# A decoder trunk's first attention on one core: TensorE's order written by hand as a pipeline over heads

## The chip, the core and the metric

The kernel runs on one core of a Trainium2 chip. Its engines work side by side, each on a list of instructions of its own: TensorE (PE) multiplies, VectorE (DVE) and ScalarE (ACT) do arithmetic on tiles, GpSimd (POOL) a little masking, and SyncE (SP) issues most DMAs. An instruction starts when those ahead of it on its engine have been issued and the semaphores that it waits for have been signalled. The metric is the device time of one execution in microseconds, lower is better.

## What is computed

One sequence of 256 tokens with 2048 features goes through two layers. Layer 0 is an attention with 32 heads of 128 that sees only the 64 best keys of each query, layer 1 a stick-breaking attention with 16 heads; behind each stands an MLP of 8192. Each of the four parts is normalised ahead and behind, shifted, scaled and gated by columns that are computed from `c` with the large weight `ada_w`. Of the reference, cut to the first attention:

```python
q_lat, c_kv, k_idx, w_idx = jnp.split(proj, [c1, c2, c3], axis=-1)   # 512, 256, 128, 16 columns
q = (q_lat @ w_qb).reshape(B, S, A_HEADS, A_QK_DIM)
q_idx = (q_lat @ w_idx_qb).reshape(B, S, IDX_HEADS, IDX_DIM)
...
score = jnp.einsum('bqsh,bqh->bqs', jax.nn.relu(dots), wb).astype(jnp.float32)
score = jnp.where(key_pos[None, None, :] <= t[None, :, None], score, -jnp.inf)
_, idx = lax.top_k(score, k_top)                                      # k_top = 64
...
logits = jnp.einsum('bqhc,bqkc->bqhk', q_abs, kv_sel).astype(jnp.float32) * scale
logits = logits + jnp.moveaxis(rel_bias[bucket], -1, 2).astype(jnp.float32)
probs = jax.nn.softmax(logits, axis=-1).astype(h.dtype)
o_lat = jnp.einsum('bqhk,bqkc->bqhc', probs, kv_sel)
return jnp.einsum('bqhc,hcv->bqhv', o_lat, w_uv)                      # then @ w_out
```

## The kernel before, in words

**Products.** Every product of fp32 values is made as three: each operand is split into a high part (ACT rounds it, L128) and a low part (DVE subtracts, L129), and high by high, low by high and high by low are added in one PSUM bank. Weights come as raw tiles of 512 KB in a ring of four (`raw`) and are split into `whi` and `wlo`, rings of four too. Beside this a `Filler` streams most of `ada_w` through DVE: each `tick` makes the steps that are due, an add of 128x1024 to `acc` (L205) or one of the "ends": a gate (two products, L244 and L245, into a bank of the tag `s`, then DVE multiplies, L246) or four transposes of columns (`col`, L215). The tag `s` has one bank, which `pT`, the gates and `col` share; `lg` has two, `av` one.

**Start.** 2048 features come in groups; `start_sum` adds the weighted rows of `ada_w` on DVE, for the last three steps one row on PE as one-column products into `col`; the column sums (L565) end a group, and then h of its features can be made (L438, L439) and multiplied with `a_w_in` (`pq`, `pk`, L602).

**Mask.** Index scores are made in `dots`; DVE then takes eight maxima at a time and strikes them out (L889, L890), eight rounds for each of the two query tiles, L891 makes the mask, POOL cuts it (L893), PE transposes it (`mt`, L899), and DVE copies it (L900). Every head's logits add the mask by products with it (L839).

**Heads.** Four heads are a group, `hq` from 0 to 7. `a_project(hq)` makes their queries (`pqT`), keys (`pkT`) and values (`pv`). `a_attend` does one head: logits `lg` (L836 two products, L839 three), bias and maximum on DVE (L844), exponentials on ACT (L849), reciprocal on DVE (L851), scaling on ACT (L854), three transposes `pT` (L857), their copy on ACT (L859), products with v, `av` (L862, L863), and the split of the result. `a_out(hq - 1, d)` makes a quarter of the output projection of the group before: 24 products `m` of 512 columns (L353 to L355), whose sum DVE adds to `y` (L387).

**Who sets the order.** At the start PE's order is written by hand (`manual_schedule`); from the first attention on, a scheduler places the instructions of every engine by the order in which the code asks for them and by its own costs. So `projected = a_project(0)` and the loop over `hq` and `hl` state what there is to do, and not where on PE it comes to stand. The second attention (`b_attend`) makes its logits in the banks `z`, waits for `e`, its exponentials, at L1076, and puts its products with v into a bank of the tag `s` (`po`, named `bo`).

Of the kernel before, what the change touches and what calls it, by code (L numbers as in the profile page):

```python
# [16 lines left out]
P = 128  # L17
# [26 lines left out]
def trunk(ctx: ExitStack, tc: tile.TileContext, x, c, rel_bias, ada_w, ada_b, norm_g, a_w_in, a_q_norm,  # L44
# [74 lines left out]
    def rows(w, k0, k1, c0, c1):  # L119
        return w.rearrange("(a p) n -> p a n", p=P)[:, k0:k1, c0:c1]  # L120
# [127 lines left out]
    class Filler:  # L248
# [61 lines left out]
        def tick(self, weight=1):  # L310
            self.due += self.per * weight
            while self.due >= 1.0:
                self.due -= 1.0
                if self.done < self.limit:
                    self.step()
# [231 lines left out]
    def start_sum(i):  # L547
        g, k, r = steps[i]
        n = SEGS[g][1]
        on_pe = 1 if i >= len(steps) - 3 else 0  # L550
# [57 lines left out]
    for i in range(len(steps) + LEAD):  # L608
# [19 lines left out]
        if waiting and not (waiting[0] in late and done < len(steps) - 3):  # L628
            for k in waiting[:1 if SEGS[g][1] == 4 else 2]:
                waiting.pop(0)  # L630
                for t in range(NT):
                    start_product(oq, (k,), t)
                    if k not in late:
                        start_product(ok, (k,), t)
        if done == 2:
            x_sums = [squares(t) for t in range(NT)]
        if done == 4:
            start_x(x_sums)
        if done == 9:
            ps = small_ps("tab", "col")  # L640
            nc.tensor.matmul(ps[:HA, :3 * P], rb, bk, start=True, stop=True)
            nc.scalar.activation(tab, ps[:HA, :3 * P], AF.Copy)
            nc.gpsimd.dma_start(out=tab_d, in_=tab)
    start_h(len(SEGS) - 1)
    waiting += range(SEGS[-1][0], NC)
# [140 lines left out]
    def a_project(hq):  # L786

        qparts = unit(rows(a_w_qb[0], 0, 4, hq * BLK, (hq + 1) * BLK), 4, BLK)
        khi, klo = a_kv_unit(uk_src, hq)
        vhi, vlo = a_kv_unit(uv_src, hq)  # L790
        qk = []
        for a in range(2):
            pf = bank("f", "pqT")
            s_piece([(k, hi[:, a * 2 * P:(a + 1) * 2 * P], lo[:, a * 2 * P:(a + 1) * 2 * P])
                     for k, (hi, lo) in enumerate(qparts)], q_of, 2, [pf], 4)
            qT = q_tile[:, hq % 2, a].rearrange("p (a t) -> p a t", a=2)
            nc.scalar.activation(qT, pf.rearrange("p (a t) -> p a t", a=2), AF.Copy, scale=QS)
# [7 lines left out]
            kT = k_tile[:, hq % 2, a].rearrange("p (a t) -> p a t", a=2)  # L805
            nc.scalar.activation(kT, pf.rearrange("p (a t) -> p a t", a=2), AF.Copy)
            qk.append((qT, kT))
        vt = []
# [3 lines left out]
        for t in range(NT):  # L812
            v = v_tile[:, hq % 2, t]
            nc.scalar.activation(v, pv[t], AF.Copy)  # L814
            vt.append(v)
        return qk, vt
# [3 lines left out]
    def a_attend(hq, hl, qk, vt):  # L820

        a, b = divmod(hl, 2)
# [3 lines left out]
        if b == 0:  # L826
# [3 lines left out]
            o_tile[0] = pair_tile((11, 16, 17, 18, 10)[(2 * hq + a) % 5], "o")  # L830
# [21 lines left out]
        for t in range(NT):  # L852
            f, _ = krng[t]
            nc.scalar.activation(lg[:, f], lg[:, f], AF.Copy, scale=rc[:, t:t + 1])  # L854
        ps = small_ps("pT")
# [3 lines left out]
        nc.scalar.activation(pT, ps[:, :3 * P], AF.Copy)  # L859
        ps = small_ps("av", "av")  # L860
        hs = slice(hl * P, (hl + 1) * P)
        nc.tensor.matmul(ps[:, :T], vt[1][:, hs], pT[:, :T], start=True, stop=False, **kw)  # L862
        nc.tensor.matmul(ps[:, P:T], vt[0][:, hs], pT[:, T:], start=False, stop=True, **kw)  # L863
        o = o_tile[0][:, b]
# [15 lines left out]
    projected = a_project(0)  # L880
# [28 lines left out]
    for hq in range(8):  # L909
        ready, projected = projected, a_project(hq + 1) if hq < 7 else None  # L910
        for hl in range(4):
            a_attend(hq, hl, *ready)
            if hq > 0:
                a_out(hq - 1, hl)
# [142 lines left out]
    def b_attend(hq, pair):  # L1057
# [22 lines left out]
        for hl, (z, e) in enumerate(zip(zs, es), pair[0]):  # L1080
            nc.scalar.activation(e, z[:, :3 * P], AF.Exp)
            po = small_ps("bo")
# [91 lines left out]
```

## Time and profile before

| | |
|---|---|
| median of 3 runs | 2440.35 us (2436.56 to 2444.9) |
| the profiled execution | 2439.51 us, its span 2437.8 |
| PE busy | 2346.0 us of the span (96%), 12320 products |
| DVE, ACT, POOL busy | 1747.3, 1229.2 and 42.5 us |

A profile shows one execution. The busy time of an engine is the sum of its records; products overlap in PE's pipeline, so a busy PE is not a PE at its peak. The start lasts until about 130 us, the mask is ready at about 205, the first attention lasts until 512, the second from about 1300 to 1690, and the MLPs fill the rest.

### The profile page before, as it was taken

Reading aid. Unit: us, or ns where it says so; the run is one execution under the profiler, and the core shown is the slowest. Engines: PE = TensorE matmul, PEld = TensorE weight load, DVE = VectorE, ACT = ScalarE, POOL = GpSimd, SP = SyncE. Lnnn points to the kernel's source line nnn. Section 1 sums busy time; section 2 is a strip of 40 time slices with the busy share of each in tenths; the row PEclk is TensorE's granted clock in tenths of the full one; section 3 lists DMA queues with packets and bytes.
Section 4 is the critical chain, followed back from the end, with each engine's and each line's share of the span. In section 5 each row is a group of like instructions: output and inputs, shape, how many; then the busy total and the mean of one; then the engine's idle time right before and its main releaser. Section 6 shows DMA issues by size and latency. Waiting matters only on the chain.

```text
span 2437.8 us, 32909 instructions
## 1 busy us (share of the span) xinstructions
PE 2346.0 (96%) x12320; PEld 1954.0 (80%) x12320; DVE 1747.3 (72%) x2221; ACT 1229.2 (50%) x1847; POOL 42.5 (2%) x74
## 2 busy tenths in 40 slices
PE   3899999999999999999999999999999999999998
PEld 2487787868888888888878988987788888888886
DVE  6789798888576876876578677887865558555556
ACT  3156555566544444445455554456654454454443
POOL 0010000000000000000000000000000000000000
PEclk9899999999999999999999999999999999999999
DMA  9987899858677877877657778895765557656554
GB/s 379 369 287 249 271 310 308 284 190 280 226 266 244 302 266 264 306 258 270 194 181 265 255 264 318 308 332 210 243 241 190 190 186 263 207 190 190 182 191 145
DMA packets 285976, 613.94 MB, mean 252 GB/s; under 512 B 19716, under 2 KB 44632, under 8 KB 285304
## 3 DMA queue, kind: packets, MB, share of 16 engines
q1 hardware_dynamic: 282688, 603.14, 72.1%
q0 software_dynamic: 2464, 8.53, 1.2%
q8 instruction: 96, 1.57, 0.2%
q14 instruction: 64, 0.52, 0.1%
q10 hardware_dynamic: 664, 0.17, 0.0%
HBM read 609.62 MB, written 2.15 MB: 251 GB/s over the span
## 4 chain that ended last, share of the span: by engine, by line
PE 78%; DMA 8%; DVE 4%; ACT 4%; issue 4%; SPq 0%; POOL 0%; DVEq 0%; POOLq 0%; ACTq 0%
PE f L944 18%; PE m L354 11%; PE m L355 11%; PE m L353 11%; PE f L946 9%; DMA w<-in_ada_w_dram 3%; DVE acc L205 1%; DMA raw<-in_a_w_out_dram 1%; DMA adaw<-in_ada_w_dram 1%; PE pv L353 1%; PE pv L354 1%; PE pv L355 1%; ACT whi L128 1%; PE pq L123 1%; PE pq L125 1%
## 5 line engine op out<-in xcount | busy, mean ns | idle before, releaser
L129 DVE TENSOR_TENSOR wlo<-raw,whi 128x1024 fp32r<-128x1024 f32 x726 | 875.9, 1221 | 423.3 <-ACT whi L128 420.8
L128 ACT ACTIVATE whi<-raw 128x1024 fp32r<-128x1024 f32 x726 | 755.7, 1056 | 800.8 <-PE f L944 311.9
L944 PE MATMUL f<-h,whi 128*128 128x512 f32 x1920 | 676.0, 394 | 0.0
L946 PE MATMUL f<-h,wlo 128*128 128x256 f32 x1920 | 543.2, 283 | 0.8 <-DVE wlo L129 0.8
L944 PEld LDWEIGHTS f<-h,whi 128*128 128x128 f32 x1920 | 360.6, 188 | 82.5
L205 DVE SCALAR_TENSOR_TENSOR acc<-adaw,cs,acc 128x1024 f32<-128x1024 f32 x300 | 384.3, 1281 | 55.0 <-DMA adaw<-in_ada_w_dram 52.1
L353 PE MATMUL m<-whi,hid 128*128 128x512 f32 x1016 | 401.4, 395 | 0.0
L355 PE MATMUL m<-wlo,hid 128*128 128x512 f32 x1016 | 401.0, 395 | 0.0
L354 PE MATMUL m<-whi,hid 128*128 128x512 f32 x1016 | 400.9, 395 | 0.0
L946 PEld LDWEIGHTS f<-h,wlo 128*128 128x128 f32 x1920 | 360.9, 188 | 2.6 <-DVE wlo L129 1.4
L355 PEld LDWEIGHTS m<-wlo,hid 128*128 128x128 f32 x1016 | 191.3, 188 | 44.6
L353 PEld LDWEIGHTS m<-whi,hid 128*128 128x128 f32 x1016 | 191.4, 188 | 44.2
L354 PEld LDWEIGHTS m<-whi,hid 128*128 128x128 f32 x1016 | 191.4, 188 | 43.1
L387 DVE TENSOR_TENSOR y<-m,y 128x512 f32<-128x512 f32 x200 | 136.8, 686 | 37.9 <-PE m L355 37.6
L353 PE MATMUL m<-whi,o 128*128 128x512 f32 x368 | 149.4, 407 | 0.5 <-ACT qkv L814 0.5
L355 PE MATMUL m<-wlo,o 128*128 128x512 f32 x368 | 146.7, 401 | 0.4 <-DVE wlo L129 0.4
L354 PE MATMUL m<-whi,o 128*128 128x512 f32 x368 | 146.7, 399 | 0.0
L205 DVE SCALAR_TENSOR_TENSOR acc<-w,cs,acc 128x512 f32<-128x512 f32 (+1 forms) x87 | 81.4, 936 | 22.9 <-DMA w<-in_ada_w_dram 20.2
L355 PEld LDWEIGHTS m<-wlo,o 128*128 128x128 f32 x368 | 69.3, 189 | 15.6 <-DVE wlo L129 1.1
L353 PEld LDWEIGHTS m<-whi,o 128*128 128x128 f32 x368 | 69.6, 189 | 13.9 <-ACT qkv L814 0.7
L354 PEld LDWEIGHTS m<-whi,o 128*128 128x128 f32 x368 | 69.5, 189 | 13.5
L123 PE MATMUL pk<-h,whi 128*128 128x256 f32 x256 | 72.8, 285 | 1.0 <-ACT q L1052 1.0
(278 smaller groups left out, 2908.2 us busy)
## 6 DMA issues: line engine op xcount, KB each, us to landing
raw<-in_mlp_w_dram SPq DMA_DIRECT2D x504, 512.0 KB, 4.4
adaw<-in_ada_w_dram SPq DMA_DIRECT2D x320, 512.0 KB, 6.2
raw<-in_b_w_in_dram SPq DMA_DIRECT2D x92, 512.0 KB, 5.3
raw<-in_a_w_out_dram SPq DMA_DIRECT2D x64, 512.0 KB, 5.8
w<-in_ada_w_dram SPq DMA_DIRECT2D x62, 512.0 KB, 9.5
raw<-in_b_w_out_dram SPq DMA_DIRECT2D x32, 512.0 KB, 7.6
raw<-in_a_w_qb_dram SPq DMA_DIRECT2D x16, 512.0 KB, 5.8
win<-in_a_w_in_dram SPq DMA_DIRECT2D x8, 912.0 KB, 9.0
```

Source lines behind the costliest of these rows:

```text
L123: nc.tensor.matmul(o, sh, mh, start=start, stop=False, skip_group_check=True)
L125: nc.tensor.matmul(o, sl, mh, start=False, stop=stop, skip_group_check=True)
L128: return (nc.scalar.activation(dst_hi, src, AF.Copy).ins, nc.vector.tensor_sub(dst_lo, src, dst_hi.bitcast(F32)).ins)
L129: nc.vector.tensor_sub(dst_lo, src, dst_hi.bitcast(F32)).ins)
L205: nc.vector.scalar_tensor_tensor(acc, w, cs[:, k:k + 1], acc, op0=ALU.mult, op1=ALU.add)
L353: nc.tensor.matmul(o, xh[:, ts_], hi, start=(k == 0), stop=False)
L354: nc.tensor.matmul(o, xl[:, ts_], hi, start=False, stop=False)
L355: nc.tensor.matmul(o, xh[:, ts_], lo, start=False, stop=(k == n - 1))
L387: nc.vector.tensor_add(y, pt[d][t], y)
L944: nc.tensor.matmul(pf[f], hi[:, fs], hb.rearrange("p a t -> p (a t)"), start=(u == 0 and i == 0), stop=False, skip_group_check=True)
L946: nc.tensor.matmul(pf[f][:, :T], lo[:, fs], hb[:, 0], start=False, stop=(u == 3 and i == 3), skip_group_check=True)
```

## The change

Ahead of the mask and of the loop PE's order is now written by hand (`manual_schedule` for PE alone, until the last output piece of the loop): products stand on PE exactly in the order in which the code asks for them. `a_project` and `a_attend` became generators: a projection has three parts (queries of the group, then keys, then values), a head has three (logits and softmax, transposes, products with v). The loop takes one head after another: logits of head n+1, transposes of head n, an output piece of the group before (or a part of the projection, where none is left), products of head n with v, a part of the projection. Beside it, a `tick` of the `Filler` makes at most one end; of the last three steps of the start only the first and the last leave a row to PE; some q products of the start stand behind the last column sums; the pair tile of a head is taken later; and in the second attention `po` is the bank `z`.

```diff
 
         def tick(self, weight=1):
             self.due += self.per * weight
-            while self.due >= 1.0:
+            begun = self.done
+            while self.due >= 1.0 and self.done < self.limit:
+                if self.steps[self.done][3] >= NC and self.done > begun:
+                    break
                 self.due -= 1.0
-                if self.done < self.limit:
-                    self.step()
+                self.step()
 
         def finish(self):
             while self.done < self.limit:
...
     def start_sum(i):
         g, k, r = steps[i]
         n = SEGS[g][1]
-        on_pe = 1 if i >= len(steps) - 3 else 0
+        on_pe = 1 if i in (len(steps) - 3, len(steps) - 1) else 0
         if k == 0:
             acc[g] = (sp.tile([P, 2 * BLK], F32, tag="acc", name=uid("acc"), bufs=2)[:, :2 * n * P],
                       bank("col", "col"))
...
             start_h(g - 1)
             waiting += range(SEGS[g - 1][0], sum(SEGS[g - 1]))
         if waiting and not (waiting[0] in late and done < len(steps) - 3):
-            for k in waiting[:1 if SEGS[g][1] == 4 else 2]:
+            for k in waiting[:1 if SEGS[g][1] == 4 or waiting[0] in late else 2]:
                 waiting.pop(0)
                 for t in range(NT):
                     start_product(oq, (k,), t)
                     if k not in late:
                         start_product(ok, (k,), t)
+            if done >= len(steps) - 3:
+                held, waiting = waiting, []
         if done == 2:
             x_sums = [squares(t) for t in range(NT)]
         if done == 4:
...
             nc.tensor.matmul(ps[:HA, :3 * P], rb, bk, start=True, stop=True)
             nc.scalar.activation(tab, ps[:HA, :3 * P], AF.Copy)
             nc.gpsimd.dma_start(out=tab_d, in_=tab)
+    for t in range(NT):
+        start_product(oq, held, t)
     start_h(len(SEGS) - 1)
-    waiting += range(SEGS[-1][0], NC)
+    waiting = range(SEGS[-1][0], NC)
     for t in range(NT):
         start_product(oq, waiting, t)
     idx_unit = lambda u: rows(a_w_idx_qb[0], 0, 4, u * BLK, (u + 1) * BLK)
...
 
     def a_project(hq):
 
-        qparts = unit(rows(a_w_qb[0], 0, 4, hq * BLK, (hq + 1) * BLK), 4, BLK)
+        both = lambda pf: pf.rearrange("p (a t) -> p a t", a=2)
+        qk, vt = ([], []), []
+        parts = unit(rows(a_w_qb[0], 0, 4, hq * BLK, (hq + 1) * BLK), 4, BLK)
+        pf = [bank("f", "pqT") for _ in range(2)]
+        s_piece([(k, hi, lo) for k, (hi, lo) in enumerate(parts)], q_of, 4, pf, 4)
+        for a in range(2):
+            qk[0].append(both(q_tile[:, hq % 2, a]))
+            nc.scalar.activation(qk[0][a], both(pf[a]), AF.Copy, scale=QS)
+        yield
         khi, klo = a_kv_unit(uk_src, hq)
-        vhi, vlo = a_kv_unit(uv_src, hq)
-        qk = []
         for a in range(2):
-            pf = bank("f", "pqT")
-            s_piece([(k, hi[:, a * 2 * P:(a + 1) * 2 * P], lo[:, a * 2 * P:(a + 1) * 2 * P])
-                     for k, (hi, lo) in enumerate(qparts)], q_of, 2, [pf], 4)
-            qT = q_tile[:, hq % 2, a].rearrange("p (a t) -> p a t", a=2)
-            nc.scalar.activation(qT, pf.rearrange("p (a t) -> p a t", a=2), AF.Copy, scale=QS)
             pf = bank("f", "pkT")
             for b in range(2):
                 for k in range(2):
...
         for t in range(NT):
             f, _ = krng[t]
             nc.scalar.activation(lg[:, f], lg[:, f], AF.Copy, scale=rc[:, t:t + 1])
+        yield
         ps = small_ps("pT")
         for i, j in enumerate((0, 2, 1)):
             nc.tensor.transpose(ps[:, i * P:(i + 1) * P], lg[:, j * P:(j + 1) * P], ident)
         pT = pT_tile[:, hl % 2, :3 * P]
         nc.scalar.activation(pT, ps[:, :3 * P], AF.Copy)
+        yield
         ps = small_ps("av", "av")
         hs = slice(hl * P, (hl + 1) * P)
         nc.tensor.matmul(ps[:, :T], vt[1][:, hs], pT[:, :T], start=True, stop=False, **kw)
         nc.tensor.matmul(ps[:, P:T], vt[0][:, hs], pT[:, T:], start=False, stop=True, **kw)
+        if b == 0:
+            o_tile[0] = pair_tile((11, 16, 17, 18, 10)[(2 * hq + a) % 5], "o")
         o = o_tile[0][:, b]
         split(o[:, 0], o[:, 1], ps[:, :T])
         o_tiles[hq].append(o)
...
     def o_of(tiles):
         return lambda k: (tiles[k][:, 0], tiles[k][:, 1])
 
-    projected = a_project(0)
+    projected = {}
+    attention_order = ExitStack()
+    attention_order.enter_context(tc.manual_schedule(engines={mybir.EngineType.PE}))
+    for _ in a_project(0):
+        pass
+    project = a_project(1)
+    next(project), next(project)
 
     for s in (slice(0, P), slice(2 * P, 3 * P)):
         nc.gpsimd.affine_select(out=score[:, s], in_=score[:, s], pattern=[[-1, P]], compare_op=ALU.is_ge,
...
         out_part(a_w_out[0], 4 * q, 4, o_of(o_tiles[q]), yt, gates.get((0, 2)), ss, d, q == 0, q == 7,
                  ("x", "f", "m")[-len(d):], **kw)
 
-    for hq in range(8):
-        ready, projected = projected, a_project(hq + 1) if hq < 7 else None
-        for hl in range(4):
-            a_attend(hq, hl, *ready)
-            if hq > 0:
-                a_out(hq - 1, hl)
+
+    heads = [divmod(h, 4) for h in range(32)]
+    outs = []
+    before = None
+    for hq, hl in heads + [(8, 0)]:
+        now = a_attend(hq, hl) if hq < 8 else None
+        if now:
+            next(now)
+        if before:
+            next(before)
+        if outs:
+            a_out(*outs.pop(0))
+        else:
+            next(project, None)
+        if before:
+            next(before, None)
+        next(project, None)
+        if hl == 0 and hq > 0:
+            outs += [(hq - 1, d) for d in range(NB)] if hq < 8 else []
+        if hl == 3:
+            for _ in project:
+                pass
+            project = a_project(hq + 2) if hq < 6 else iter(())
+        before = now
+    for o_ in outs:
+        a_out(*o_)
+    attention_order.close()
     filler.finish()
     a_out(7, 0)
     early = {}
...
         oo = pair_tile(8 + hq % 2 * 2 + pair[0] // 2, "o")
         for hl, (z, e) in enumerate(zip(zs, es), pair[0]):
             nc.scalar.activation(e, z[:, :3 * P], AF.Exp)
-            po = small_ps("bo")
+            po = z
             hs = slice(hl * P, (hl + 1) * P)
             nc.tensor.matmul(po[:, :T], vt[0][:, hs], e[:, :T], start=True, stop=False, **kw)
             nc.tensor.matmul(po[:, P:T], vt[1][:, hs], e[:, T:], start=False, stop=True, **kw)
```

Three places show how PE's list moves. The names are those of the program (`pqT` queries and `pkT` keys of a group, `lg` logits, `pT` transposes, `av` products with v, `gate` an end of the `Filler`, `m` output), with tile numbers; line numbers of the kernel after are larger by 2 to 16.

The first place is on PE at the mask's transposes `mt`. Before:

```order
L124 MATMUL pqT_1729<-qlat,whi_1660 128x256
L125 MATMUL pqT_1729<-qlat,wlo_1661 128x256
L899 LDWEIGHTS misc
L899 MATMUL mt_1369<-ident_b,misc 128x128
L899 LDWEIGHTS misc
L899 MATMUL mt_1369<-ident_b,misc 128x128
L899 LDWEIGHTS misc
L899 MATMUL mt_1369<-ident_b,misc 128x128
L123 MATMUL pqT_1729<-qlat,whi_1664 128x256
```

and after:

```order
L124 MATMUL pkT_1411<-ckv_711,whi_1384 128x256
L125 MATMUL pkT_1411<-ckv_711,wlo_1385 128x256
L915 LDWEIGHTS misc
L915 MATMUL mt_1486<-ident_b,misc 128x128
L915 LDWEIGHTS misc
L915 MATMUL mt_1486<-ident_b,misc 128x128
L915 LDWEIGHTS misc
L915 MATMUL mt_1486<-ident_b,misc 128x128
L842 MATMUL lg_1503<-qkv_709,qkv_708 128x128
```

Before, the transposes stand in the midst of the third group's queries (`hq` 2), 42 products of which are ahead of them; after, they stand right behind the second group's keys (`hq` 1), and the logits of head 0 follow.

The second place is on PE in the first heads, which have no output piece beside them. Before, from the transposes of head 1 on:

```order
L857 MATMUL pT_1583<-ident,lg_716 128x128 x3
L862 MATMUL av_1588<-lg_717,qkv_713 128x256
L863 MATMUL av_1588<-lg_717,qkv_713 128x128
L857 MATMUL pT_1611<-ident,lg_716 128x128 x3
L836 MATMUL lg_1863<-qkv_712,qkv_711 128x128
L836 MATMUL lg_1863<-qkv_712,qkv_711 128x256
L839 LDWEIGHTS misc
L839 MATMUL lg_1863<-big_flip,misc 128x128
L839 LDWEIGHTS misc
```

and after, from the transposes of head 0 on:

```order
L864 MATMUL pT_1564<-ident,lg_713 128x128 x3
L870 MATMUL av_1569<-lg_714,qkv_710 128x256
L871 MATMUL av_1569<-lg_714,qkv_710 128x128
L244 MATMUL gate_1575<-ahl_1529,ones_r 128x256
L245 MATMUL gate_1575<-ahl_1529,ones_r 128x256
L842 MATMUL lg_1583<-qkv_709,qkv_708 128x128
L842 MATMUL lg_1583<-qkv_709,qkv_708 128x256
L845 LDWEIGHTS misc
L845 MATMUL lg_1583<-big_flip,misc 128x128
L845 LDWEIGHTS misc
L845 MATMUL lg_1583<-big_flip,misc 128x128
L845 LDWEIGHTS misc
```

Before, the logits of heads 2 and 3 stand further ahead, and two heads' transposes follow each other closely; after, one head's transposes and its products with v are neighbours, with the next head's logits behind them.

The third place is on PE where a `gate` meets an attention head, in the third group. Before:

```order
L354 MATMUL m_2286<-whi_2275,o_1936 128x512
L355 MATMUL m_2286<-wlo_2276,o_1936 128x512
L862 MATMUL av_2255<-lg_717,qkv_713 128x256
L863 MATMUL av_2255<-lg_717,qkv_713 128x128
L244 MATMUL gate_2260<-ahl_2132,ones_r 128x256
L245 MATMUL gate_2260<-ahl_2132,ones_r 128x256
L836 MATMUL lg_2313<-qkv_712,qkv_711 128x128
```

and after, twice:

```order
L845 MATMUL lg_2176<-big_flip,misc 128x128
L864 MATMUL pT_2192<-ident,lg_713 128x128 x3
L244 MATMUL gate_2211<-ahl_2121,ones_r 128x256
L245 MATMUL gate_2211<-ahl_2121,ones_r 128x256
L355 MATMUL m_2218<-whi_2201,o_1847 128x512
```

```order
L870 MATMUL av_2246<-lg_714,qkv_710 128x256
L871 MATMUL av_2246<-lg_714,qkv_710 128x128
L244 MATMUL gate_2252<-ahl_2215,ones_r 128x256
L245 MATMUL gate_2252<-ahl_2215,ones_r 128x256
L244 MATMUL gate_2265<-ahl_2256,ones_r 128x256
L245 MATMUL gate_2265<-ahl_2256,ones_r 128x256
L123 MATMUL pkT_2272<-ckv_711,whi_2261 128x256
```

Before, the gate stands behind `av`; after, one stands right behind `pT`, in whose bank it writes, and two stand behind each other.

## Rows read from the trace of the kernel before

**Rows 1.** The page's busy times: us (share of the span) x instructions.

```profile
PE 2346.0 (96%) x12320; PEld 1954.0 (80%) x12320; DVE 1747.3 (72%) x2221; ACT 1229.2 (50%) x1847; POOL 42.5 (2%) x74
```

**Rows 2.** Windows: stretch, length, each engine's busy time, granted clock, DMA share, GB/s.

```profile
178.00:204.60 26.60, 25.05 (x181) 23.14 (x179) 25.64 (x64) 15.56 (x22) 0.30 (x2) 1.00 0.77 265
204.60:223.30 18.70, 15.94 (x104) 12.83 (x104) 15.55 (x46) 14.73 (x41) 2.73 (x5) 1.00 0.51 154
223.30:512.00 288.70, 279.51 (x1527) 230.20 (x1527) 250.86 (x426) 169.94 (x346) 8.37 (x12) 1.00 0.87 297
555.00:1260.00 705.00, 705.00 (x3531) 593.71 (x3530) 507.69 (x553) 342.04 (x439) 2.02 (x4) 1.00 0.76 262
1300.00:1690.00 390.00, 380.68 (x2487) 344.75 (x2486) 296.35 (x311) 195.30 (x246) 2.11 (x5) 1.00 0.83 294
```

**Rows 3.** The timeline at the mask: start, duration, engine, line, out<-in [idle before].

```profile
203.87 0.36 DVE L891 TENSOR_SCALAR misc<-misc 128x384 bf16<-128x384 f32 x1
...
204.65 0.53 PE L899 MATMUL mt<-ident_b,misc 128*128 128x128 bf16 x3 [1.25 <-POOL misc L893]
```

**Rows 4.** Waits of PE, 223.3 to 512: us in total, times, longest.

```profile
PE av L862 <- ACT lg L859: 2.9, 5, 1.1
PE pT L857 <- ACT lg L854: 2.7, 5, 1.5
...
PE col L215 <- DVE mod L216: 0.6, 1, 0.6
```

**Rows 5.** PE's timeline behind the mask.

```profile
205.19 0.28 PE L124 MATMUL pqT<-qlat,whi 128*128 128x256 f32 x1
...
205.31 0.28 PE L125 MATMUL pqT<-qlat,wlo 128*128 128x256 f32 x1
...
211.30 0.40 PE L353 MATMUL pv<-whi,ckv 128*128 128x512 f32 x1
211.53 0.39 PE L354 MATMUL pv<-whi,ckv 128*128 128x512 f32 x1
...
223.25 0.50 PE L353 MATMUL m<-whi,o 128*128 128x512 f32 x1 [0.47 <-ACT qkv L814]
```

**Rows 6.** The timeline of one head, later in the first attention.

```profile
289.92 0.29 DVE L844 CUSTOM_DVE_ANT_0 lg<-lg,bias 128x128 f32<-128x128 f32 x1
...
290.48 1.22 DVE L129 TENSOR_TENSOR wlo<-raw,whi 128x1024 fp32r<-128x1024 f32 x1
...
291.81 0.40 ACT L849 ACTIVATE lg<-lg,st 128x128 f32<-128x128 f32 x1 [2.27 <-DVE st L846]
...
293.07 0.81 ACT L854 ACTIVATE lg<-lg,rc 128x128 f32<-128x128 f32 x2 [0.27 <-DVE rc L851]
...
293.73 0.27 PE L857 MATMUL pT<-ident,lg 128*128 128x128 f32 x1
...
294.08 0.38 PE L857 MATMUL pT<-ident,lg 128*128 128x128 f32 x2
...
294.90 0.47 ACT L859 ACTIVATE lg<-pT 128x384 f32<-128x384 f32 x1
```

**Rows 7.** The granted clock: two windows (columns as in rows 2).

```profile
72.10:75.20 3.10, 0.00 (x0) 0.00 (x0) 2.35 (x4) 2.95 (x9) 0.00 (x0) 1.00 1.09 386
75.60:79.00 3.40, 3.40 (x5) 1.55 (x6) 3.26 (x6) 0.19 (x1) 0.00 (x0) 0.50 1.09 389
```

**Rows 8.** The timeline at the end of the start.

```profile
112.09 3.90 DVE L205 SCALAR_TENSOR_TENSOR acc<-w,cs,acc 128x512 f32<-128x512 f32 x5 [0.92 <-DMA w<-in_ada_w_dram]
112.48 5.38 PE L602 MATMUL pq<-win,h 128*128 128x512 f32 x8
...
120.76 0.16 DVE L587 SCALAR_TENSOR_TENSOR mod_start<-col,g_col 128x2 f32<-128x2 f32 x1 [4.77 <-PE col L565]
...
121.62 1.22 PE L602 MATMUL pq<-win,h 128*128 128x512 f32 x1 [0.91 <-DVE h L439]
```

**Rows 9.** Waits of PE in the second attention, 1300 to 1690 (columns as in rows 4).

```profile
PE z L1076 <- DVE e L1075: 8.2, 8, 2.3
```

More of the change, by code (lines that the diff above doesn't have):

```diff
@@ L804, in a_project @@
                         xh, xl, start=(b == 0 and k == 0), stop=(k == 1))
[L805 to L808, printed above, removed]
+            qk[1].append(both(k_tile[:, hq % 2, a]))
+            nc.scalar.activation(qk[1][a], both(pf), AF.Copy)
+        yield
+        vhi, vlo = a_kv_unit(uv_src, hq)
         pv = [bank("m", "pv") for _ in range(NT)]
@@ L812, in a_project, with a_attend @@
         for t in range(NT):
[L813 to L816, printed above, removed]
+            vt.append(v_tile[:, hq % 2, t])
+            nc.scalar.activation(vt[t], pv[t], AF.Copy)
+        projected[hq] = list(zip(*qk)), vt
     biases, o_tile = {}, {}
-    def a_attend(hq, hl, qk, vt):
+    def a_attend(hq, hl):
+        qk, vt = projected[hq]
         a, b = divmod(hl, 2)
@@ L829, in a_attend @@
                                                                  ap=[[1, P], [3 * P, 2], [1, T]]))
-            o_tile[0] = pair_tile((11, 16, 17, 18, 10)[(2 * hq + a) % 5], "o")
         bias = biases[0][:, a]
@@ L859, in a_attend @@
         nc.scalar.activation(pT, ps[:, :3 * P], AF.Copy)
+        yield
         ps = small_ps("av", "av")
```

## The prediction, made before the change was run

> **What bounds the kernel now.** The page's head says that TensorE (PE) is busy for 2346.0 of 2437.8 us [rows 1], so the end can come nearer only by PE's idle time or by fewer products; the change removes no product to speak of. I therefore cut the span into windows, to see where PE idles in the stretch that the change rewrites [rows 2]. From 178 to 512 us, the mask and the first attention, it idles 1.55 us ahead of the mask's transposes (26.60 less 25.05), 2.76 between them and the first output product, and 9.19 in the rest of the attention. The two MLPs have nothing to give: 705.00 busy in 705.00 us in the first. The second attention idles 9.3 of 390. So 13.5 us of visible idle time is what a better order in the first attention can win.
>
> Next I asked what PE waits for. Ahead of the mask it is VectorE (DVE): the top-64 search ends at 203.87, GpSimd masks, and the mask's transposes start on PE at 204.65 [rows 3]. DVE is busy 25.64 of 26.60 us there [rows 2], so PE's order cannot bring this point forward; it decides only how much PE has done before it. Behind the mask the two largest waits are av for ACT's copy of pT (2.9 us in 5 times) and pT for ACT's scaled logits (2.7 in 5) [rows 4]; the rest are single ones of about 1 us and less.
>
> Third, the price of a product. Starts stand 0.12 us apart for 256 columns and 0.23 for 512 [rows 5]. A record lasts longer (0.39 for 512 columns), so a wait hides up to 0.16 us under the record before it: with some 25 waits behind the mask, 4 us beside the 11.95 that windows show, 16 in all.
>
> **The change part by part.** The sum is made against the profiled execution, 2439.5 us; the median of the runs is 0.8 above it.
>
> *Work that no longer lies ahead of the mask.* In the order of before the mask's transposes stand behind all of the second head group's projections and more than half of the third's queries; in that of after they stand right behind the second group's queries and keys, the two pieces that were asked for by name. Counted, 72 products move behind the mask: 42 queries and 12 keys of the third group, of 256 columns (54 x 0.12 = 6.4 us), 12 of the second group's values, of 512 columns (12 x 0.23 = 2.8), and the logits of one head in 4 pieces (about 0.7); 2 gate products move ahead of it (-0.2). Together 9.6 us. What hid them was DVE's search; PE's idle time there grows from 1.55 to about 11 us, and the same products stand on the path afterwards: **+9.6**. DVE's list up to the end of the search is nearly the same (one wlo of 1.2 us less, three small ones of 1.6 more), so the mask itself comes within -0.4 and +1.2 of where it was: 0.
>
> *First heads.* The order behind the mask is now lg(0), gate, pv, lg(1), pT(0), av(0), lg(2), pT(1), av(1) and so on; until head 3 nothing long stands between, since there is no output piece yet. One head shows its chain [rows 6]: DVE starts the sum with the bias at 289.92, a wlo of 1.22 us comes between, exponentials start at 291.81, the scaling starts at 293.07 and lasts 0.81; pT follows at 293.73, and its copy ends at 295.37. That is 4 us from logits to pT and 1.6 from pT to av. PE has 1 us of logits and at most 2.8 of pv to cover the first, and nothing for the second. Walked head by head with these durations, PE waits 8.9 us before pT(3). Before, it waited 2.76, or 3.7 with what records hide: **+5**. Bounds: 1, if DVE's queue holds no long add between a head's steps, and 8, if an acc of 1.28 stands ahead of the sum and of the reciprocal in each of the heads.
>
> *The clock.* After PE had idled for 3.1 us at 72.1, the granted clock was 0.50 in the next 3.4 us, half of 2.4 GHz, though PE was busy throughout [rows 7]. Behind the mask, with 15.94 busy of 18.7 us in many short pieces, it stayed at 1.00 [rows 2]. An idle time of 11 us ahead of the mask is longer than the 3.1 that lowered it, so I expect the low level when the mask arrives. What the 3.4 us at 75.6 held would have taken half at full speed; here PE's work is short pieces between waits, so that more of it runs low, and a part hides in the waits. **+4**, from 0 (the idle time is broken up and the clock stays) to 11 (it stays low until the first output products). The Trainium skill, "TensorE: Matmul & The Clock Gate", section "HAM oscillation — how this bites in real kernels", has the same rule: an engine left idle between pieces is throttled to half its clock, and each next piece starts cold. The trace agrees with it at 72.1. By that rule alone the sum would get the upper end, 11, instead of 4, since the first heads are idle gaps and short pieces.
>
> *Steady heads.* From head 4 on a head is lg(n+1), pT(n), 24 output products (24 x 0.23 = 5.6 us), av(n), then a piece of projection. The output piece covers the 1.6 us between pT and av; from logits to pT there are av, the piece of projection and the 5.6 us of the head before, against the 4 us of [rows 6] and somewhat more where DVE's or ACT's queue is longer (pT's longest wait is 1.5 now). So the 2.9 and 2.7 us of [rows 4] should go: **-5.6**, from 0 (other waits take their place) to -9.2, all of the idle time in that window.
>
> *Gate and column products behind transposes.* They write to the one bank that pT uses too. In the order of after a gate or a col stands right behind pT twice each, a gate stands right behind another gate once, and 8 col in a row twice, seven places in all. Each must wait until ACT has copied pT or DVE has read the last one; pT's last transposes end at 294.46, its copy at 295.37 [rows 6], and with the signals there and back I take 1.3 us: seven are 9.1 us, of which before had 0.6 (a col behind a col, [rows 4]), and some 1.5 hide under PE's records and other waits: **+7**. Bounds 2 (the copies are done sooner, and waits for them shift what would wait anyway) and 10.
>
> *Start.* The last but one step's row moves from PE to DVE, and some q products move behind the last column sums. PE now spends 5.38 us on 8 products at 112.48, the column sums come behind them, and DVE has waited 4.77 us for them at 120.76; the next product starts at 121.62 [rows 8]. Four one-column products fewer (0.5) and the q products behind the sums shorten that; a fifth add of 0.78 (3.90 / 5) on DVE lengthens its own chain, which has slack. **-2**, from -3 to +1.
>
> *Second attention.* The output of a pair now goes into the z bank, and its products can follow at once; the output products between z and the next use of e get fewer for four of five pairs that changed. Those waits are 8.2 us in 8 times now [rows 9]; some 3 products fewer (0.7 us) in four places: **+2**, from -2 to +5. The one step per tick of the ada stream spreads gates and costs nothing by itself: DVE is idle 13% of the steady window [rows 2].
>
> Sum: 9.6 + 0 + 5 + 4 - 5.6 + 7 - 2 + 2 = +20, so 2459.5.
>
> **The rivals.**
> *Faster.* A hand order that always has long work behind each softmax step could remove every wait behind the mask: 16 us gained and 2 at the start, against 9.6 of work that lost its cover: 2431. It decides if gates and columns find their bank free and the first heads wait no more than before. For it speaks that the steady cover of 5.6 us is over the 1.6 to av; against it that the first four heads have no output piece at all.
> *The same.* The steady heads win 8, the start 2, and gates cost only 2, the clock nothing, the first heads 1: +9.6 + 1 - 8 - 2 + 2 = +2.6, some 2441.
> *Full clock, small stalls.* The idle time ahead of the mask is broken up, and the first heads and gates go by their lower bounds: +9.6 + 1 - 5.6 + 5 - 2 + 2 = +10: 2450.
> *Low clock throughout.* The first heads run low until the first output product and each waits for an add on DVE: 11 for 4, 8 for 5, and 10 + 5 for 7 + 2 elsewhere would be +36; not all at once, so 2474.
>
> **How the numbers follow.** About 7.3 us, 0.3%, is what a measurement of this kernel can tell from no change. The main case (2450 to 2470 as its own range) has 0.45, the low clock 0.14, full clock with small stalls 0.13: slower 0.72. The same has 0.18, since the +9.6 is sure by the order and the -5.6 by the waits, and the rest is of either sign. Faster has 0.10: all that it needs is bounded by 16 us of idle time. The range leaves out the faster case and the upper part of the low clock: 2438 to 2476.
>
> **What would show it.** Right: PE idles 9 us or more in the 25 us ahead of the mask's transposes, with a granted clock near 0.5 after them; first output product 25 to 35 us behind the mask (18.6 now); pT and av waits nearly gone later, gate and col waits of about 1.3 us in their place. Wrong: a mask that comes much earlier or later than 202 to 205; PE busy ahead of the mask as before; or gate waits under 0.5 us, which would take the sum to 2454, and with a full clock to 2450.

## The result, and the profile after

The changed kernel takes 2461.31 us (median of 6 runs, 2457.17 to 2463.74), the kernel before 2440.04 (6 runs): ratio 1.0083, 95% interval 1.007 to 1.0096. The forecast was 2459.5 in a range of 2438 to 2476, 72% for slower. The total fits to 2 us; its terms fit less well, and two large misses nearly cancel.

The busy times of the page after [rows 1]; the same work, 21.3 us more span:

```profile
span 2459.1 us, 32922 instructions
...
PE 2343.6 (95%) x12312; PEld 1959.8 (80%) x12312; DVE 1748.0 (71%) x2222; ACT 1230.8 (50%) x1847; POOL 42.3 (2%) x74
```

The first reading is where on the way the two part. I read the start of the same products in both timelines (us):

| start of | before | after | difference |
|---|---|---|---|
| first index product | 133.66 | 133.71 | 0.0 |
| mask's transposes | 204.65 | 205.27 | +0.6 |
| first output product | 223.25 | 236.74 | +13.5 |
| first product of the MLP | 565.68 | 574.54 | +8.9 |
| first z of the second attention | 1345.62 | 1354.96 | +9.3 |
| last products with v there | 1665.7 | 1686.9 | +21.2 |
| last output product | 2427.78 | 2449.04 | +21.3 |

So some 13 us are lost right behind the mask, 5 are won back in the rest of the first attention, and 12 are lost again in the second attention, where I had forecast 2.

The timeline of PE after at the mask, which answers to [rows 3], and the first output product [rows 5]:

```profile
205.27 0.64 PE L915 MATMUL mt<-ident_b,misc 128*128 128x128 bf16 x3 [13.42 <-POOL misc L909]
...
236.74 0.48 PE L355 MATMUL m<-whi,o 128*128 128x512 f32 x1
```

PE waits 13.42 us for the mask instead of 1.25, and the first output product comes 31.5 us behind it instead of 18.6. Windows after, for [rows 2] and [rows 7]:

```profile
178.00:204.60 26.60, 13.85 (x106) 13.12 (x104) 25.36 (x63) 11.10 (x17) 0.00 (x0) 0.86 0.70 240
...
191.90:205.20 13.30, 0.00 (x0) 0.00 (x0) 11.90 (x39) 2.37 (x4) 0.28 (x2) 0.70 0.41 131
205.20:210.70 5.50, 5.43 (x19) 4.35 (x20) 1.93 (x9) 1.40 (x5) 0.26 (x2) 0.50 0.01 3
210.70:214.00 3.30, 2.67 (x18) 2.04 (x16) 0.96 (x5) 3.16 (x6) 0.00 (x0) 0.99 0.00 0
```

PE did 25.05 us of work ahead of the mask, now 13.85. The granted clock is 0.50 while PE works without a break from 205.2 to 210.7, and back at 0.99 behind that: 5.43 us at half of 2.4 GHz cost some 2.7.

Waits of PE from the first output product on, after (us in total, times, longest); they answer to [rows 4]:

```profile
PE hT L455 <- ACT xn L452: 3.5, 2, 2.7
PE col L215 <- DVE mod L216: 3.1, 2, 1.5
PE gate L244 <- ACT lg L866: 1.7, 2, 1.0
PE col L215 <- ACT lg L866: 1.5, 2, 0.8
PE pv L355 <- ACT y L387: 1.4, 1, 1.4
PE gate L244 <- DVE gg L246: 1.2, 1, 1.2
```

No pT and no av is left: the pipeline over heads does what it says, once there are output pieces. In their place stand gate and col products (7.5 us), which wait for ACT's copy of pT (L866) or for DVE's read of the one ahead: all users of one bank.

Waits of PE in the second attention after, for [rows 9]:

```profile
PE z L1113 <- DVE e L1112: 8.5, 8, 2.9
PE pk L123 <- ACT whi L128: 3.3, 1, 3.3
PE z L1121 <- ACT e L1118: 3.2, 3, 1.2
PE m L355 <- ACT whi L128: 2.4, 2, 1.6
PE m L357 <- DVE wlo L129: 0.8, 2, 0.5
PE pq L125 <- DVE wlo L129: 0.2, 1, 0.2
```

The 8.2 us that were there are 8.5; new are the waits for weights (whi, wlo) and for ACT at the products with v (L1121). The rows sum to 18.4 us, where before had 9.2 (8.2 at z, 1.0 at pk). Behind the longest of them the granted clock is 0.51 from 1490.8 to 1494.2 with PE busy for 3.12 us, so half of that, some 1.6, comes on top: 10.8 of the 11.9 us that this stage grew by.

### The profile page after: what moved, and what is told of

The parts are those of the page before. It is cut to its first block, busy times and chain, and to the rows that moved or that the text cites. A ratio compares the mean times of both kernels' runs of the same rounds, so it can differ in the third digit from the quotient of the medians.

```text
span 2459.1 us, 32922 instructions
## 1 busy us (share of the span) xinstructions
PE 2343.6 (95%) x12312; PEld 1959.8 (80%) x12312; DVE 1748.0 (71%) x2222; ACT 1230.8 (50%) x1847; POOL 42.3 (2%) x74
## 4 chain that ended last, share of the span: by engine, by line
PE 79%; DMA 7%; issue 4%; DVE 4%; ACT 4%; SPq 1%; POOL 0%; DVEq 0%; POOLq 0%; ACTq 0%
PE f L981 18%; PE m L357 12%; PE m L356 12%; PE m L355 12%; PE f L983 9%; DMA w<-in_ada_w_dram 3%; DMA adaw<-in_ada_w_dram 3%; DVE acc L205 2%; DMA raw<-in_b_w_out_dram 1%; ACT whi L128 1%; DVE wlo L129 1%; PE pv L355 1%; PE pv L356 1%; PE pv L357 1%; PE pq L123 1%
## 5 line engine op out<-in xcount | busy, mean ns | idle before, releaser
L205 DVE SCALAR_TENSOR_TENSOR acc<-adaw,cs,acc 128x1024 f32<-128x1024 f32 x300 | 384.4, 1281 | 61.4 <-DMA adaw<-in_ada_w_dram 58.3
L983 PEld LDWEIGHTS f<-h,wlo 128*128 128x128 f32 x1920 | 361.0, 188 | 2.0 <-DVE wlo L129 0.9
L389 DVE TENSOR_TENSOR y<-m,y 128x512 f32<-128x512 f32 x200 | 136.9, 686 | 31.8 <-PE m L357 31.5
L205 DVE SCALAR_TENSOR_TENSOR acc<-w,cs,acc 128x512 f32<-128x512 f32 (+1 forms) x88 | 82.2, 934 | 23.0 <-DMA w<-in_ada_w_dram 20.2
L355 PEld LDWEIGHTS m<-whi,o 128*128 128x128 f32 x368 | 69.4, 188 | 17.5 <-ACT whi L128 3.2
L356 PEld LDWEIGHTS m<-whi,o 128*128 128x128 f32 x368 | 69.4, 189 | 14.3
```

Of the source, the lines that this page charges most:

```text
L205: nc.vector.scalar_tensor_tensor(acc, w, cs[:, k:k + 1], acc, op0=ALU.mult, op1=ALU.add)
L355: nc.tensor.matmul(o, xh[:, ts_], hi, start=(k == 0), stop=False)
L356: nc.tensor.matmul(o, xl[:, ts_], hi, start=False, stop=False)
L389: nc.vector.tensor_add(y, pt[d][t], y)
L983: nc.tensor.matmul(pf[f][:, :T], lo[:, fs], hb[:, 0], start=False, stop=(u == 3 and i == 3), skip_group_check=True)
```

## The experiments

Each kernel is named by its label. The first four try the second attention, which went most against the forecast, and the work ahead of the mask. "Less than after" is the difference of two medians that were not taken side by side; each had runs of before beside it. By the ratios to these the differences are 7.3 us for a_tick, 11.2 for a_first, 6.1 for a_gate, 7.8 for a_fill3 and 25.6 for combo3.

**a_bo**: the kernel after, with the edit of the second attention undone.

```diff
-            po = z
+            po = small_ps("bo")
```

> The kernel after, with the one edit in the second attention undone: the products with v go into a bank of their own again (bo). The profiles show the second attention 12 us longer after the change, where I had forecast 2. Theory Z: this edit makes it so, since the products with v now stand right behind the last product into z and wait for ACT's exponential (3.2 us of such waits, none before) and hold the z bank longer; then the time falls from 2461 to about 2451, and the waits of z for e at the products with v are gone. Rival S: the second attention lost time because the stream of ada_w and the weights meet it in another state (PE waits there 3.3 and 2.4 us for whi, none before), by the rule of one end per tick; then this kernel stays at 2459 to 2462.

Measured: 2462.85 (4 runs), ratio to before 1.0106 (1.0081 to 1.013). Nothing won: theory Z falls.

**b_z**: the kernel before, with that edit alone.

> The kernel before, with the edit of the second attention alone (products with v into the z bank). Theory Z: 2440 becomes about 2450. Rival S: 2439 to 2443, and the waits for whi in the second attention do not appear.

Measured: 2440.17 (10 runs), ratio 1.0003 (0.9988 to 1.0018). The edit costs nothing either way.

**a_tick**: the kernel after, with the loop of `tick` of before.

> The kernel after, with the rule of one end per tick taken out. Theory Z: no gain in the second attention; the first attention gets more ends behind each other, each waiting 1 to 1.7 us for the one bank, so 2461 to 2466. Rival S: the waits for whi in the second attention go, 2449 to 2455.

Measured: 2450.15 (5 runs), ratio 1.0053 (1.0028 to 1.0079): 11 us less, though the interval touches that of after. From the first z to the last product with v the second attention takes 320.1 us, as before (320.1); after it takes 331.9. PE waits for no weights there. Rival S holds.

**a_fill**: the second group's values, the third group's queries and the first products of two heads' logits asked for ahead of the mask.

```diff
-    next(project), next(project)
+    for _ in project:
+        pass
+    project = a_project(2)
+    next(project)
...
+    for hl in range(2):
+        begun.append(a_attend(0, hl))
+        next(begun[hl])
     ps = small_ps("mt").bitcast(BF16)
```

> The kernel after, with the work put ahead of the mask again that stood there before: values of the second group, queries of the third group (their copies behind the logits of head 3), and the first two products of the logits of heads 0 and 1. If the idle time ahead of the mask is what it cost (9.2 us of products moved behind it and some 2.7 us of half clock), the time falls by 8 to 12 us, to about 2451: PE then idles some 4 us ahead of the mask instead of 13.4. Rival: the products moved were cover for the first heads, whose waits for ACT then grow by as much as is won (values between the logits of heads 0 and 1 are 2.8 us, the queries behind the transposes of head 3 5.7 us): under 4 us won.

Measured: 2469.78 (4 runs), ratio 1.0134 (1.0116 to 1.0152), slower than after, against both theories. PE's timeline of a_fill says why:

```profile
227.30 0.64 PE L927 MATMUL mt<-ident_b,misc 128*128 128x128 bf16 x3 [21.25 <-POOL misc L917]
```

The mask comes 22 us later. The scheduler still sets DVE's order and puts first what the program asks for first; with the projections ahead of the search, more of DVE's other work stands among its 16 rounds. From the first round to the mask DVE does 16 adds of the stream instead of the 3 of after, 10 low parts instead of 7, and 3 gates instead of 1. Before, the projections were asked for behind the search and only PE ran them early. The experiment had moved DVE's work too, so it says nothing yet on PE's cover.

**a_first**: the rule of one end per tick only up to the end of the first attention.

```diff
-                if self.steps[self.done][3] >= NC and self.done > begun:
+                if self.one and self.steps[self.done][3] >= NC and self.done > begun:
...
     attention_order.close()
+    filler.one = False
```

> The kernel after, with the rule of one end per tick kept in the first attention and taken out behind it. The run without the rule anywhere gave 2450 and lost only 2.6 us in the second attention, while three runs with the rule and the hand order lost 14 to 16 there. Theory R (the rule in the second attention bunches the adds of ada_w and holds up the weights): 2461 becomes 2447 to 2451. Rival E (the second attention only loses what it meets from the first attention's order of ends): 2457 to 2462.

Measured: 2448.65 (10 runs), ratio 1.0037 (1.0023 to 1.0052): 12.7 us less than after. The rule behind the first attention is that loss. PE's waits in the second attention of a_first:

```profile
PE z L1116 <- DVE e L1115: 7.5, 8, 2.1
PE pk L123 <- ACT q L1092: 0.3, 1, 0.3
```

No wait for weights or at the products with v is left, though these still use the bank z. Over all runs, from the first z to the last product with v: 330.9 to 336.3 us in the seven traces that have the rule there (after, a_bo, a_fill, a_gate, a_warm, a_fill3, a_start), 317 to 324 in the seven that have not.

What the rule does there is seen in DVE's adds (L205), in windows of after (length, busy, count, clock, DMA share, GB/s):

```profile
1350.00:1410.00 60.00, 6.76 (x6) 1.00 0.65 216
1410.00:1470.00 60.00, 16.93 (x14) 1.00 0.77 270
1470.00:1530.00 60.00, 16.67 (x13) 0.97 0.82 285
1530.00:1590.00 60.00, 23.06 (x18) 1.00 0.90 314
1590.00:1690.00 100.00, 34.57 (x27) 1.00 0.85 305
```

and of a_first, which reaches the stage 3 us later:

```profile
1350.00:1410.00 60.00, 10.03 (x8) 0.97 0.71 240
1410.00:1470.00 60.00, 15.62 (x13) 1.00 0.75 263
1470.00:1530.00 60.00, 23.12 (x19) 1.00 0.90 325
1530.00:1590.00 60.00, 21.54 (x17) 1.00 0.85 312
1590.00:1690.00 100.00, 28.41 (x23) 1.00 0.86 313
```

A tick that makes an end stops at the next end, so the adds behind four ends are put off by some ticks: 33 against 40 are done by 1530. They come later in runs, and their fetches with them. ACT's and SP's timelines of after at the longest wait (pk, 3.27 us, at 1491):

```profile
1483.77 1.06 ACT L128 ACTIVATE whi<-raw 128x1024 fp32r<-128x1024 f32 x1 [1.72 <-DMA raw<-in_b_w_in_dram]
1489.97 1.06 ACT L128 ACTIVATE whi<-raw 128x1024 fp32r<-128x1024 f32 x1 [5.14 <-DVE acc L205]
```

```profile
1478.31 0.39 SPq L103 DMA_DIRECT2D raw<-in_b_w_in_dram  x1
1480.22 2.66 SPq L268 DMA_DIRECT2D adaw<-in_ada_w_dram  x2
1482.93 0.43 SPq L103 DMA_DIRECT2D raw<-in_b_w_in_dram  x1
```

A raw tile stands in SP's list behind two fetches of the stream, each of which waits until an add frees its tile. It is issued at 1482.93 and takes 7.0 us to land; the high part starts 0.1 us behind the landing, 5.14 us after the end of the one before it, and PE waits 3.27. (The row names an add as releaser of the high part; that add ends at the same moment, but it is the landing that ACT waits for.)

```profile
1491.08 0.58 PE L123 MATMUL pk<-h,whi 128*128 128x256 f32 x1 [3.27 <-ACT whi L128]
```

ACT's waits of high parts for an add or for the landing of a raw tile sum to 52.6 us in the second attention of after, to 27.3 in a_first, 26.0 in a_tick and 31.9 before. Those put down to an add alone do not tell the kernels apart: 14.3 in after, but 11.9 in a_tick too, which loses nothing there. That the rule costs the 12 us is shown by the runs; that it does so by SP's list and not by DVE's time is argued from these rows, and no run parts the two.

**a_gate**: gates and columns of the first attention alternate between the banks of pT and av.

```diff
+    def end_ps(name):
+        if not turn:
+            return small_ps(name)
+        turn[0] = "av" if turn[0] == "s" else "s"
+        return small_ps(name, turn[0])
...
-        ps = small_ps("gate")[:, :T]
+        ps = end_ps("gate")[:, :T]
```

> The kernel after, with gates and columns of the first attention written alternately to the bank of av or of pT, whichever was not used last. PE's stalls of gate and col products that stand behind a transpose or behind each other sum to 8.6 us in the trace after (1.6 before). Theory B (they wait for the one bank): 5 to 8 us less, 2453 to 2457. Rival: they wait for their operand or the time is taken back by the next wait of the head: under 2 us.

Measured: 2453.4 (5 runs), ratio 1.0058 (1.0034 to 1.0082): 7.9 us less, but the interval overlaps that of after (1.007 to 1.0096). PE's waits of a_gate from 230 to 570:

```profile
PE col L221 <- DVE o L129: 3.8, 3, 1.9
...
PE gate L250 <- DVE o L129: 0.9, 1, 0.9
PE gate L251 <- DVE ahl L129: 0.2, 1, 0.2
```

Of 7.5 us 4.9 are left, where an end now waits for the split of av. From the mask's transposes to the MLP's first product this trace takes 3.8 us less than after (365.5 and 369.3). The traces of a_bo and a_first, with PE's order of after in this stretch, take 366.7 and 368.4, so that 1 to 4 us are placed there; the rest I could not place.

**a_warm**: PE kept busy ahead of the mask.

```diff
     next(project), next(project)
+    warm = bank("av", "warm")
+    for _ in range(95):
+        nc.tensor.matmul(warm[:, :T], ckv[:, 0, 0, :P], ckv[:, 0, 0], start=True, stop=True, skip_group_check=True)
```

> The kernel after, with 95 more products of 256 columns, read by nobody, between the second group's keys and the mask's transposes, to keep PE busy through the 13.4 us in which it waits. They take 11.3 us at 0.119 each. Clock theory: the first 5.4 us behind the mask no longer run at half clock, and the time falls by 2 to 3 us, with a granted clock of 1.00 from 204 to 212. Rival: the half clock is hidden in waits of the first heads: 0 to 1.

Measured: 2460.06 (4 runs, 2450.81 to 2467.04), ratio 1.0096 (1.0062 to 1.0129), too wide to tell 2 us. In the trace, the fastest of the four runs, the first output product stands 28.3 us behind the mask's transposes instead of 31.5, 3.2 less, about the size that the theory has. That it is the clock is not shown: PE's waits for ACT in this stretch are 2.7 us (av 2.0, pT 0.7) instead of 5.6, which is 2.9 of the 3.2, and the clock is not at full speed throughout:

```profile
201.20:206.00 4.80, 4.50 (x18) 3.60 (x19) 1.93 (x9) 1.40 (x5) 0.47 (x2) 0.64 0.00 0
206.00:212.00 6.00, 5.07 (x32) 3.85 (x30) 3.33 (x13) 5.45 (x14) 0.00 (x0) 1.00 0.05 16
```

**a_fill3**: a_fill with the search first in the program, and the stream held until the mask is copied.

```diff
-    project = a_project(1)
...
+            if self.hold:
+                return
...
+    filler.hold, filler.cap = True, 3
+    project = a_project(1)
```

> As the kernel a_fill, but the search for the mask comes first in the program's order and the stream of ada_w is held until the mask is copied (then at most three steps per tick), so that DVE's list up to the mask is that of before with two more low parts (2.4 us). Its predecessor lost because DVE did 12 more adds and 3 more gates ahead of the mask, which came 22.6 us late. If lost cover ahead of the mask is what the hand order cost: mask at 205 to 208, PE idle under 6 us ahead of it, and 5 to 9 us less than after, 2452 to 2456. If the products moved were needed as cover for the first heads: 2458 to 2463.

Measured: 2451.92 (7 runs), ratio 1.0051 (1.0034 to 1.0067): 9.4 us less than after. PE's timeline of a_fill3 at the mask:

```profile
203.93 0.64 PE L932 MATMUL mt<-ident_b,misc 128*128 128x128 bf16 x3 [4.85 <-POOL misc L916]
```

The mask is on time, PE idles 4.85 us instead of 13.42, and 8.6 less idle gives 9.4 less time (7.8 by the ratios), 9.3 of it from the mask to the MLP's first product (360.0 and 369.3): the work ahead of the mask is worth its full price. A granted clock of 0.50 stands behind these 4.85 us too (203.8 to 210).

**combo3**: a_fill3, a_gate and the rule of one end per tick in the first attention only.

> The hand order with its three costs taken out together: work ahead of the mask as in a_fill3 (9.4 us less by itself), gates and columns of the first attention alternating between two banks (8 less), one end per tick only in the first attention (12.7 less). If the three are separate causes they add: 2461 - 30 = 2431, some 9 us under the kernel before, ratio 0.995 to 0.998. If they share a cause (all are DVE's order), two of them are worth little once one is taken out: 2437 to 2445, the same as before.

Measured: 2435.12 (12 runs), ratio 0.9978 (0.9965 to 0.999): faster than both kernels, by 0.2% against before, and 26 of the 30 us. The work ahead of the mask and the rule add (22 us by themselves). Whether the banks add, the times cannot say: by the ratios the three sum to 25.1 and combo3 has 25.6, with intervals of 3 to 6 us each. In the traces they gave little: from the mask to the MLP combo3 takes 360.0 us, as a_fill3 does, since a second gate that goes to av's bank waits 4.5 us at 274 for the split of av.

**a_start**: the kernel after with the edits of the start undone.

> The kernel after with the edits of the start undone (three rows on PE again, no q products held back). My forecast put these edits at -2 us: then 2463. The two profiles show the first index product at 133.66 before and 133.80 after, that is 0: then 2461. Other profiles of these kernels have it from 128.8 to 134.4, so that under 2 us may not be told apart.

Measured: 2458.27 (6 runs), ratio 1.0081 (1.0062 to 1.0099), not to be told from after (1.0083); the interval does not exclude the 2 us of the forecast either.

**combo3w** and **combo4**: combo3 with 42 more products ahead of the mask, and that with two gates behind av both in the bank of pT.

```diff
+    warm = bank("av", "warm")
+    for _ in range(42):
+        nc.tensor.matmul(warm[:, :T], ckv[:, 0, 0, :P], ckv[:, 0, 0], start=True, stop=True, skip_group_check=True)
     ps = small_ps("mt").bitcast(BF16)
```

> The kernel combo3 with 42 more products of 256 columns, read by nobody, ahead of the mask's transposes, in the 5 us in which PE waits there. The profile of combo3 still shows the half clock behind that wait. Clock theory: granted clock 1.00 behind the mask and 1.5 to 3 us less between the mask and the first output product than the 24.3 of combo3. Rival: those pieces wait for the softmax anyway, under 1 us.

> The kernel combo3w with two gates behind products with v both in the bank of pT: in combo3 the second of them went to av's bank and waited 4.6 us at 274 for the split of av, which stood late in DVE's queue. If that wait is on the path: 2 to 4 us less than combo3w, in all 2428 to 2432, ratio to before 0.995 to 0.997. Rival: the wait for the first gate's read takes its place: within 1.5 us of combo3w.

Measured: 2439.61 (12 runs), ratio 1.0 (0.9988 to 1.0012), and 2439.87 (11 runs), 1.0003 (0.9992 to 1.0014). Both miss. In the traces the first output product stands 23.6 us behind the mask in combo3w, 24.3 in combo3: under 1 us, the rival. The clock theory is not cleanly tried: behind the mask the granted clock of combo3w is 1.00 until 212.8, but 0.51 from there to 216.3, behind waits of 0.45, 2.56 and 0.58 us. The second gate of combo4 still waits 3.5 us, now for DVE to read the first one: the rival. The 4.5 us lost against combo3 lie in the second attention, where nothing was edited: 323.9 us from its first z to its last product with v against 317.4. By operation, tile name and shape the rows of DVE and of ACT stand in the same order in both traces; what differs is when they come. Ahead of the exponentials ACT splits a sum of the stream and waits 4.22 us for it at 1347.4 (0.95 in combo3), since DVE's last adds of it, behind waits for their fetches, start 3.7 us later (1341.02 against 1337.34). PE's first wait for e is 4.37 us instead of 1.33, and behind it the granted clock is 0.50 from 1352.9 to 1359.7 with PE busy for 5.11 us, where combo3 has 1.00. The wait is 3.0 and half of the 5.11 some 2.6 of the 6.5 us. Why the fetches land later is not shown.

## Why the prediction was right, and where it was not

- **Work that lost its cover, +9.6**: right. PE's idle time ahead of the mask went from 1.25 to 13.42 us, and a_fill3 got 9.4 back.
- **Mask, 0**: +0.6.
- **First heads, +5**: about +3. In after their waits for ACT are 5.6 us (pT 3.2, av 2.4), before PE idled 2.76 in that stretch. The walk had PE wait too long (8.9 us); which of its steps, I have not taken apart.
- **Clock, +4**: about +2.7, by 5.43 us at the low level. The rule of the Trainium skill that the prediction named ("TensorE: Matmul & The Clock Gate", section "HAM oscillation — how this bites in real kernels") agrees in kind: the clock was low behind the idle time. As the prediction read it, each short piece would have begun cold, 11 us; the trace shows the full clock again at 210.7, in the midst of the first heads' pieces, and it stays although PE waits 0.58 to 1.96 us five times behind that. In a_first and a_start, with the same order on PE, it did fall again, to 0.51 from 221.9 to 228.8 and to 0.50 from 219.2 to 226.0, and the first output product came 32.7 us behind the mask instead of 31.5. That the low clock costs 2.7 us is worked out from its length and not shown by a run: a_warm's time cannot tell 2 us.
- **Steady heads, -5.6**: the direction was right, the size too small. From the mask to the MLP the stretch grew by 8.2 us (369.3 less 361.0, by the table of starts); the other terms in it sum to 9.6 + 3 + 2.7 + 7 = 22, so the steady heads won some 14 by what is left over. Counted directly, the time from the start of a product to that of the pT or av behind it, less the pitch of the former (0.23 us for 512 columns, 0.12 for 256, 0.11 for 128), sums to 17.5 us before and to 5.5 after from the first output product to the MLP: 12 won. I had held the visible idle time (9.19) to be the bound. It is not: the rows show only 5.6 of the 17.5 us, for a wait of up to 0.16 us hides below the record of an output product. I had counted this for the rival and left it out of the term.
- **Gates and columns, +7**: right as counted: 7.5 us of such waits where 0.6 was. What taking them away is worth is less sure: 1 to 4 us in a_gate's stretch, 6 to 8 in its time, the interval of which overlaps that of after.
- **Start, -2**: 0 in the profiles, and a_start cannot tell 2 us. Over all traces the first index product starts between 129.0 and 134.6 us.
- **Second attention, +2**: the step that failed, twice. It measured 12. The edit that I priced, the products with v in z, is worth nothing (b_z, a_bo). The edit that I put at nothing, "spreads gates and costs nothing by itself: DVE is idle 13%", costs 11 to 13 (a_first). I had taken DVE's mean idle time in the first attention as cover for a stage that came later, and had not asked what a skipped add holds back: the stream's next fetch and, as argued above, behind it in SP's list the next weights.

The sum came out since -6 to -8 in the steady heads and +10 in the second attention nearly cancel; that the total fits to 2 us is luck to this extent, while the direction rests on the work ahead of the mask, which a_fill3 shows. Two sums of the rivals were off without bearing on this: the same is 2442 and not 2441, and full clock, small stalls took 5 for the gates, whose lower bound was 2. The rivals: the faster one failed on the gates and the first heads, as it had been said; "low clock throughout" did not happen.

## What to carry to other kernels

An order by hand on one engine takes from the scheduler what it did for free, here work put into a wait; and since the other engines are still scheduled by the program's order, asking for that work earlier by hand moves their work too, unless the wait's own chain is asked for first. Where several products share one bank, who used the bank last decides what they wait for; moving some to another bank moved the wait to that bank's reader, and its gain is not clear of noise here. A rule that makes a background stream skip a turn can be paid in a later stage, here 12 us in the second attention; that it is paid where the stream's fetches and the main fetches share a queue is argued, not shown.

## What the runs showed of the hardware that was not expected

PE's visible idle time is no bound of what an order can win: the waits of pT and av showed 5.6 us, and 12 were won. And the granted clock fell to 0.50 behind an idle time of 4.85 us (a_fill3) as behind one of 13.42, and for 3.4 us behind one of 1.84 with PE busy before it (a_warm, 0.64 in 4.8 us), and so it did in combo3w, behind waits of at most 2.56, while the 1.25 us of the kernel before left it at 1.00; what decided between these short ones stays open.
